# The low part of a weight granule by an accumulating DMA instead of a subtraction on VectorE

## The chip, the cores and the metric

The kernel runs on one core of a Trainium2 chip. The metric is device time in microseconds; the median of three runs of the kernel before is 964.5 us (963.53 to 964.99). TensorE is called PE here (its weight loads PEld), VectorE DVE, ScalarE ACT, GpSimd POOL, and SyncE, which issues most DMAs, SP.

## The reference

One layer of a hybrid decoder for 512 tokens of width 1024, all in float32. The input is normalised, shifted and scaled to `h`; one wide projection gives the inputs of two mixers (a chunkwise mLSTM with 4 heads, a differential attention with 8) and of their gates; both are normalised, gated, projected and merged.

```python
h = rmsnorm(x, norm_g[l]) * (1.0 + scale[:, None]) + shift[:, None]
proj = h @ w_in[l]
(qm, km, vm, om, zm, im, fm, qa, ka, va, za, gm, ga) = jnp.split(proj, split_idx, axis=-1)
...
ym = hm @ w_proj_m[l]
...
ya = ha @ w_proj_a[l]
y = jax.nn.sigmoid(gm) * ym + jax.nn.sigmoid(ga) * ya
x = x + gate[:, None] * (y @ w_out[l])
return rmsnorm(x, final_g)
```

## The kernel before

Products are made from a high and a low part of each operand. The high part is the float32 value rounded to the type that PE reads (float32r), the low part is the value less its high part; three products (high by high, high by low, low by high; lines 135 to 137, `mm3`) stand for one in float32.

Weights come in granules of 128 x 1024 numbers (512 KB). A granule of `w_in` is 128 columns and the whole contraction (`proj_b`, 24 products of 512 columns) or 256 columns and half the contraction (`proj_v`, 48 products of 256 columns); those of the two output projections are of the same size (`attn_proj`, `proj_m`). The first eight granules of `w_in` belong to the first two attention heads and are split by code of their own (lines 581 to 617). The other 128 go through `split_granule` (line 149): SP loads `raw` (line 146), ACT casts it to `whi` (line 100), DVE subtracts `whi` from `raw` and writes `wlo` (line 118). Each of the three tiles has three buffers in the pool `stg`, so a granule can be prepared while PE works on the two before it. The eight granules of `w_out` are split at the end of the kernel by `out_weights`, which calls `split` itself.

The program is written in the order of the granules; the attention heads and the mLSTM run as generators beside it and hand in a piece of work at each `tick`. A scheduler of the framework then sets each engine's queue by readiness and priority (the split of a granule is emitted at high priority), and each engine works its queue in order. POOL has little to do: masks on the bias tiles (`bt`, line 224) and on the mLSTM's weights (`wt`, line 766), and some memsets (`sw`, line 461).

Of the kernel before, what the change touches and what calls it, by code (L numbers as in the profile page):

```python
# [9 lines left out]
F32 = mybir.dt.float32  # L10
F32R = mybir.dt.float32r
AF = mybir.ActivationFunctionType
ALU = mybir.AluOpType
# [3 lines left out]
P = 128  # L17
# [18 lines left out]

# granules of the combined input projection, in the order of use: ("B", col) covers 128
# columns and the whole contraction, ("A", col, half) 256 columns and half the contraction,
# ("F", k) the columns of the first pair of attention heads and one block of the contraction
def _granules():  # L40
# [25 lines left out]
def hybrid_block_kernel(ctx: ExitStack, tc: tile.TileContext, xT, x, c, wada2, wada, win, wif, wpm, wpa, wout,  # L66
# [41 lines left out]

    # not before what is being emitted now on the same engine
    def pin(inst, eng):  # L110
# [4 lines left out]
    def split(hi, lo, src, eng="act", scale=None):  # L115
        copy_r(eng, hi, src, scale)
        if scale is None:
            recent["dve"] = nc.vector.tensor_tensor(lo, src, hi.bitcast(F32), ALU.subtract)  # L118
        else:
            nc.vector.scalar_tensor_tensor(lo, src, scale, hi.bitcast(F32), ALU.mult, ALU.subtract)  # L120

    # products of the heads keep their order of issue among themselves; the projections fill in
    last = [None]
# [20 lines left out]
    def load_granule(src):  # L144
        raw = stg.tile([P, D], F32, tag="raw", name=nm("raw"))
        nc.sync.dma_start(raw, src)
        return raw

    def split_granule(src):
        raw = load_granule(src)  # L150
        hi = stg.tile([P, D], F32R, tag="whi", name=nm("whi"))
        lo = stg.tile([P, D], F32R, tag="wlo", name=nm("wlo"))
        with tc.high_priority():
            split(hi, lo, raw, eng="act")
        return hi, lo
# [11 lines left out]

# [1 line left out]
    crow = stg.tile([1, D], F32, tag="raw", name="crow")  # L169
# [23 lines left out]

    # 1 / sqrt(scale * ms + eps) times -2 / scale: table value and one Newton step
    def rstd(ms_ps, scale, r=None, in_turn=None):
# [32 lines left out]

# [1 line left out]
    # silu(c) on every partition, in halves  # L230
    csl = sb.tile([P, D], F32, tag="v", bufs=2, name="csl")
    csl_done = []
    idle = core_ps()

    # products without a reader: the clock of the array stays up while the input is on its way
    def keep_warm(n, after=None):
# [24 lines left out]

    # the table of the reciprocal root comes in while x is on its way
    warm = const.tile([P, 1], F32, name="warm")
# [14 lines left out]

    # the vector engine takes its part of what leads to a block of h in this order
    mod_last = [x_sum]  # L280
# [34 lines left out]

    # x times -norm_g / 2, one block of the columns
    def x_gain(k):
# [6 lines left out]

# [1 line left out]
    toe_d = dram.tile([AH, P, RL], F32, name="toe_d")  # L326
# [11 lines left out]
    h_lo = const.tile([P, NK, S], F32R, name="h_lo")  # L338
    # out^T block: 128 columns of the projection on partitions, tokens along the free axis
    def proj_b(col, between=None):  # L340
# [23 lines left out]

    # tokens on partitions, 256 columns along the free axis; hi and lo parts [P, 4, 256]
    def proj_v(col, half, pss):
# [17 lines left out]

# [1 line left out]
    KOFF = {0: 0, 1: 512, 3: 896, 2: 1152}  # L386
    QOFF = [0, 128, 384, 768]
    LO, HI = slice(0, 64), slice(64, 128)

    # per map m the high and low parts of -q/8 stacked on the partitions; the high part at 64 m  # L390
    def evac_qa(ps):
# [7 lines left out]

    # the high part of k on both halves of the partitions, and the low parts of the two maps  # L400
    def evac_ka(ps):
# [96 lines left out]

# [1 line left out]
    acol = const.tile([P, NT * MH], F32, name="acol")  # L500
    me_d = dram.tile([MH, 2 * S], F32, name="me_d")

    def if_gates():
        # columns 0: f, 32: i, 64: low part of f, 96: low part of i
        wraw = stg.tile([P, D], F32, tag="raw", name="wraw_if")
# [20 lines left out]
        for _ in range(2):  # L526
            yield
        # tokens on the partitions for what follows
        ps = core_ps()
# [5 lines left out]
        yield  # L535
        # log_sigmoid(f) = min(f, 0) - log1p(exp(-|f|)), log1p(e) = 2 atanh(e / (2 + e))
        nc.scalar.activation(e, f, AF.Abs)
# [37 lines left out]

# [1 line left out]
    fq = [acc_ps() for _ in range(2)]  # L577
# [71 lines left out]

    # merge gates: 1 + tanh is twice the sigmoid; they wait in DRAM  # L650
    gt_d = dram.tile([16, P, S], F32, name="gt_d")
# [14 lines left out]

# [1 line left out]
    for p in range(1, 4):  # L668
# [18 lines left out]

    # half the gate as a row in DRAM
    gate_d = dram.tile([8, P], F32, name="gate_d")
# [6 lines left out]

# [1 line left out]
    ya_d = dram.tile([8, P, S], F32, name="ya_d")  # L698
# [12 lines left out]

# [1 line left out]
    JOFF = [0, 512, 896, 1152]  # L713
# [42 lines left out]
    def mlstm_core(h, q, k, v, hv):  # L756
        # stabilised weights exp(a_s - M_t), zero for s > t
        mt = sb.tile([P, S], F32, tag="me", bufs=2, name=nm("mt"))
        et = sb.tile([P, S], F32, tag="me", bufs=2, name=nm("et"))
        nc.sync.dma_start(mt, me_d[h:h + 1, 0:S].to_broadcast([P, S]))  # L760
        nc.sync.dma_start(et, me_d[h:h + 1, S:2 * S].to_broadcast([P, S]))
        wt = sb.tile([P, 1408], F32, tag="p", bufs=PB, name=nm("wt"))
        for j in range(NT):
            w = S - JT[j]
            ws = wt[:, JOFF[j]:JOFF[j] + w]
            nc.gpsimd.affine_select(ws, mt[:, JT[j]:S], [[1, w]], ALU.is_ge, BIG, base=JT[j] - P * j,
                                    channel_multiplier=-1)
            nc.scalar.activation(ws, ws, AF.Exp, scale=-1.0, bias=acol[:, j * MH + h:j * MH + h + 1])
        yield
        sw = sb.tile([P, 2, 1408], F32R, tag="sw", name=nm("sw"))  # L770
        sh, sl = sw[:, 0, :], sw[:, 1, :]
        for j in range(NT):
            w = S - JT[j]
            js = slice(JOFF[j], JOFF[j] + w)
            ps = core_ps()
            jb = slice(j * P, j * P + P)
            for kk in range(2):
                mm3(ps[:, 0:w], (k[kk][0][:, jb], k[kk][1][:, jb]), (q[kk][0][:, JT[j]:S], q[kk][1][:, JT[j]:S]),
                    kk == 0, kk == 1, head=True)
            nc.vector.tensor_mul(wt[:, js], ps[:, 0:w], wt[:, js])  # L780
            split(sh[:, js], sl[:, js], wt[:, js], eng="act")
            if j > 0:
                nc.vector.tensor_add(wt[:, JT[j]:S], wt[:, JT[j]:S], wt[:, js])
            yield
        dh, dl = tmp(dt=F32R), tmp(dt=F32R)
        split(dh, dl, wt[:, 0:S], eng="dve")
        yield
        ps = out_ps()
        inorder(nc.tensor.matmul(ps, ones_r, dh, start=True, stop=False))
        inorder(nc.tensor.matmul(ps, ones_r, dl, start=False, stop=True))  # L790
        rd = sb.tile([P, S], F32, tag="me", bufs=2, name=nm("rd"))
        nc.scalar.activation(rd, ps, AF.Abs)
        nc.vector.tensor_max(rd, rd, et)
        nc.vector.reciprocal(rd, rd)
        while len(v) < 2:
            yield
        for d in range(4):
            ps = out_ps()
            vd = slice((d % 2) * P, (d % 2) * P + P)
            for j in range(NT):  # L800
                js = slice(JOFF[j], JOFF[j] + S - JT[j])
                mm3(ps[:, JT[j]:S], (v[d // 2][0][:, j, vd], v[d // 2][1][:, j, vd]), (sh[:, js], sl[:, js]),
                    j == 0, j == NT - 1, head=True)
            t = sb.tile([P, S], F32, tag="z", bufs=8, name=nm("h"))
            nc.vector.tensor_mul(t, ps, rd)
            hv.append(t)
            yield
# [21 lines left out]

    # ym becomes what the other heads and the attention branch bring to the merge  # L830
    def premerge(b, g):
# [8 lines left out]

    # the output weights stay on chip; the input h makes room for some of them
    wo = [None] * NK
# [18 lines left out]

    # the projection of the head before, as its parts come up
    def fill():
# [53 lines left out]

# [1 line left out]
    gf = sb.tile([P, 2, D], F32, tag="v", bufs=2, name="gf")  # L919
# [142 lines left out]
```

## Time and profile before

| | |
|---|---|
| runs | 964.99, 963.53, 964.50 us |
| span of the profiled execution | 960.5 us |
| its granted TensorE clock, mean | 0.997 |
| busy: PE, DVE, ACT, POOL | 947.8, 603.9, 457.3, 17.0 us |
| DMA | 114.95 MB, mean 120 GB/s |

The profiled execution is one of its own; its span runs from the first to the last instruction, and its time around that span isn't told. The three runs lie 3.0 to 4.5 us above the span, the median 4.0 us. In the rows, "[1.2 <-ACT whi]" at the end of a line is idle time of the engine before the instruction and what ended it; a DMA share is the mean busy share of the core's 16 DMA engines.

### The profile page before, as it was taken

What the parts mean: (1) busy time and instruction counts of PE and PEld (TensorE: products, weight loads), DVE (VectorE), ACT (ScalarE), POOL (GpSimd) and SP (SyncE); (2) the same over time, 40 slices, a digit from 0 to 9 for tenths busy, and PEclk for the clock granted to TensorE, in tenths of its full rate; (3) what the DMA queues carried; (4) which work ended last, traced back from release to release, by engine and by line L of the source; (5) the groups of instructions that cost most, each with busy time, mean ns of one, the idle gap of its engine ahead of it and who ended that gap; (6) DMA issues with size and microseconds to landing.
All of it is one profiled execution on the core that took longest, in us unless ns stands there. A gap on an engine that the chain in (4) does not pass through costs nothing.

```text
span 960.5 us, 12250 instructions
## 1 busy us (share of the span) xinstructions
PE 947.8 (99%) x4735; PEld 782.3 (81%) x4735; DVE 603.9 (63%) x975; ACT 457.3 (48%) x741; POOL 17.0 (2%) x40
## 2 busy tenths in 40 slices
PE   7999999999999999999999999999999999999997
PEld 4886877887787788888888888898888888888886
DVE  7965777867755537433648535486554876738944
ACT  7455776766556644322336333363223642226422
POOL 0000000000001000000000000000000000000000
PEclk9999999999999999999999999999999999999999
DMA  9871313333422243342222222223132234335421
GB/s 346 308 226 67 116 66 109 128 132 121 131 78 88 87 166 111 132 141 100 88 89 88 89 87 100 76 89 109 68 109 69 86 110 148 118 129 203 148 67 66
DMA packets 40659, 114.95 MB, mean 120 GB/s; under 512 B 8289, under 2 KB 8553, under 8 KB 39578
## 3 DMA queue, kind: packets, MB, share of 16 engines
q1 hardware_dynamic: 40010, 113.11, 35.1%
q10 hardware_dynamic: 592, 1.07, 0.4%
q8 instruction: 37, 0.61, 0.3%
q14 instruction: 20, 0.16, 0.1%
HBM read 106.78 MB, written 10.00 MB: 122 GB/s over the span
## 4 chain that ended last, share of the span: by engine, by line
PE 97%; DMA 1%; ACT 1%; DVE 0%; SPq 0%; issue 0%
PE acc L135 27%; PE acc L136 27%; PE acc L137 26%; PE core L135 4%; PE core L136 4%; PE core L137 4%; PE core L439 2%; PE core L438 2%; PE core L468 1%; DMA relt<-in_relb_dram 1%; DMA xt<-in_xT_dram 0%; PE core L238 0%; PE core L488 0%; PE core L489 0%; SPq L174 0%; PE core L331 0%
## 5 line engine op out<-in xcount | busy, mean ns | idle before, releaser
L135 PE MATMUL acc<-h_hi,whi 128*128 128x512 f32 x688 | 274.4, 399 | 0.3 <-DVE qk L407 0.3
L118 DVE TENSOR_TENSOR wlo<-raw,whi 128x1024 fp32r<-128x1024 f32 x129 | 157.7, 1223 | 179.4 <-ACT whi L100 171.3
L100 ACT CAST whi<-raw 128x1024 fp32r<-128x1024 f32 x129 | 135.3, 1049 | 282.6 <-PE acc L136 224.3
L136 PE MATMUL acc<-h_lo,whi 128*128 128x512 f32 x656 | 259.4, 395 | 0.0
L137 PE MATMUL acc<-h_hi,wlo 128*128 128x512 f32 x656 | 259.1, 395 | 0.0
L135 PEld LDWEIGHTS acc<-h_hi,whi 128*128 128x128 f32 x688 | 129.0, 188 | 32.5 <-issue 1.5
L137 PEld LDWEIGHTS acc<-h_hi,wlo 128*128 128x128 f32 x656 | 123.0, 187 | 29.9
L136 PEld LDWEIGHTS acc<-h_lo,whi 128*128 128x128 f32 x656 | 123.1, 188 | 27.5 <-issue 0.4
L135 PE MATMUL acc<-whi,h_hi 128*128 128x256 f32 x352 | 99.6, 283 | 0.0
L137 PE MATMUL acc<-whi,h_lo 128*128 128x256 f32 x352 | 98.9, 281 | 0.0
L136 PE MATMUL acc<-wlo,h_hi 128*128 128x256 f32 x352 | 98.8, 281 | 0.0
L136 PE MATMUL acc<-hl,whi 128*128 128x512 f32 x192 | 74.8, 390 | 0.0
L135 PE MATMUL acc<-hh,whi 128*128 128x512 f32 x192 | 74.8, 390 | 0.0
L137 PE MATMUL acc<-hh,wlo 128*128 128x512 f32 x192 | 74.8, 389 | 0.0
L135 PEld LDWEIGHTS acc<-whi,h_hi 128*128 128x128 f32 x352 | 66.3, 188 | 1.8 <-issue 0.8
L136 PEld LDWEIGHTS acc<-wlo,h_hi 128*128 128x128 f32 x352 | 66.3, 188 | 0.7
L137 PEld LDWEIGHTS acc<-whi,h_lo 128*128 128x128 f32 x352 | 66.3, 188 | 0.0
L441 DVE CUSTOM_DVE_ANT_0 pt<-core,bt 128x128 f32<-128x128 f32 (+3 forms) x64 | 30.3, 487 | 30.1 <-PE core L439 29.9
L443 ACT ACTIVATE pt<-pt,mn 128x128 f32<-128x128 f32 (+3 forms) x64 | 35.6, 558 | 19.8 <-DVE mn L441 19.3
L137 PEld LDWEIGHTS acc<-hh,wlo 128*128 128x128 f32 x192 | 36.1, 188 | 7.6
L135 PEld LDWEIGHTS acc<-hh,whi 128*128 128x128 f32 x192 | 36.1, 188 | 7.4
L136 PEld LDWEIGHTS acc<-hl,whi 128*128 128x128 f32 x192 | 36.1, 188 | 7.3
(276 smaller groups left out, 1362.0 us busy)
## 6 DMA issues: line engine op xcount, KB each, us to landing
raw<-in_win_dram SPq DMA_DIRECT2D x112, 512.0 KB, 3.4
wa<-in_wada_dram SPq DMA_DIRECT2D x8, 1024.0 KB, 7.0
raw<-in_wpm_dram SPq DMA_DIRECT2D x16, 512.0 KB, 3.4
raw<-in_wada_dram SPq DMA_DIRECT2D x8, 512.0 KB, 3.3
raw<-in_wpa_dram SPq DMA_DIRECT2D x8, 512.0 KB, 3.5
raw<-in_wout_dram SPq DMA_DIRECT2D x8, 512.0 KB, 3.2
gt_d<-tmp SPq DMA_DIRECT2D x12, 256.0 KB, 2.2
toe_d<-rev_d SPq DMA_DIRECT2D x8, 320.0 KB, 6.4
```

Source lines behind the costliest of these rows:

```text
L100: recent["act"] = nc.scalar.copy(dst, src)
L118: recent["dve"] = nc.vector.tensor_tensor(lo, src, hi.bitcast(F32), ALU.subtract)
L135: a = nc.tensor.matmul(ps, lhs[0], rhs[0], start=start, stop=False)
L136: b = nc.tensor.matmul(ps, lhs[l[0]], rhs[l[1]], start=False, stop=False)
L137: c = nc.tensor.matmul(ps, lhs[r[0]], rhs[r[1]], start=False, stop=stop)
L438: inorder(nc.tensor.matmul(ps, q[m][:, qs], kh[m][:, 0:wn], start=True, stop=False))
L439: inorder(nc.tensor.matmul(ps, q[m][a, qs], kl[a, 0:wn], start=False, stop=True))
L441: nc.vector.tensor_tensor_reduce(pp, ps[:, 0:w], bt[:, S - w:S], 1.0, BIG, ALU.add, ALU.min, mn[:, qb, m:m + 1])
L443: nc.scalar.activation(pp, pp, AF.Exp, scale=-1.0, bias=mn[:, qb, m:m + 1], accum_out=ls[:, qb, m:m + 1])
L468: inorder(nc.tensor.transpose(ps[:, n:n + P], pt[:, 0, o:o + P], ident))
```

## The change

In `split_granule` the call of `split` is taken apart. ACT casts `raw` to `whi` as before. Then ACT writes the negated high part into `wlo` (an activation with scale -1), and a DMA that POOL issues reads the same granule from DRAM a second time and adds it onto `wlo`. DVE's subtraction is gone, and `raw` has one reader left. The eight granules of the first heads and those of `w_out` are split as before. Comments are taken out elsewhere, and lines behind 157 have numbers that are higher by 3.

```diff
     def split_granule(src):
         raw = load_granule(src)
         hi = stg.tile([P, D], F32R, tag="whi", name=nm("whi"))
         lo = stg.tile([P, D], F32R, tag="wlo", name=nm("wlo"))
         with tc.high_priority():
-            split(hi, lo, raw, eng="act")
+            recent["act"] = nc.scalar.copy(hi, raw)
+            nc.scalar.activation(lo, hi.bitcast(F32), AF.Copy, scale=-1.0)
+            nc.gpsimd.dma_start(lo, src, accum_op=ALU.add)
         return hi, lo
```

ACT's queue before, from the first granule behind the first heads (`qk` are the parts of the first heads' queries and keys, `acc` the PSUM banks that they are read from, `v` the values):

```order
L100 CAST whi_663<-raw_661 128x1024
L395 ACTIVATE qk_576<-acc_198 64x512
L395 ACTIVATE qk_579<-acc_198 64x512
L405 CAST qk_583<-acc_200 64x512
L406 CAST qk_583<-acc_200 64x512
L100 CAST v_606<-core_202 128x512
L100 CAST v_606<-core_203 128x512
L405 CAST qk_587<-acc_200 64x512
L100 CAST whi_729<-raw_727 128x1024
L406 CAST qk_587<-acc_200 64x512
```

The second granule's cast stands between the two casts of `qk_587`.

The same piece of ACT's queue now (L155 is the cast of a granule, L156 the negation):

```order
L155 CAST whi_663<-raw_661 128x1024
L398 ACTIVATE qk_576<-acc_198 64x512
L156 ACTIVATE wlo_664<-whi_663 128x1024
L398 ACTIVATE qk_579<-acc_198 64x512
L408 CAST qk_583<-acc_200 64x512
L409 CAST qk_583<-acc_200 64x512
L100 CAST v_606<-core_202 128x512
L100 CAST v_606<-core_203 128x512
L408 CAST qk_587<-acc_200 64x512
L409 CAST qk_587<-acc_200 64x512
L155 CAST whi_730<-raw_728 128x1024
```

A negation has come between the first two L398, and the second granule's cast now follows the pair of casts of `qk_587`.

POOL's queue before, in the later attention heads (`bt` is a head's bias tile, `sw` holds a head's transposed weights, `wt` the mLSTM's):

```order
L224 AFFINE_SELECT bt_2745<-bt_2745 128x128
L461 MEMSET sw_2312 128x2x128
L461 MEMSET sw_2663 128x2x128
L461 MEMSET sw_2990 128x2x128
L766 AFFINE_SELECT wt_3783<-mt_3779 128x512
```

It goes from head to head with nothing between.

The same place in POOL's queue now (L157 is the accumulating DMA):

```order
L227 AFFINE_SELECT bt_2775<-bt_2775 128x128
L157 DMA wlo_2089<-in_win_dram 128x1024
L157 DMA wlo_2153<-in_win_dram 128x1024
L464 MEMSET sw_2336 128x2x128
L157 DMA wlo_2204<-in_win_dram 128x1024
L157 DMA wlo_2250<-in_win_dram 128x1024
L157 DMA wlo_2298<-in_win_dram 128x1024
```

The DMAs of the granules stand between the masks and memsets, so each waits for what POOL has ahead of it.

## Rows read from the trace of the kernel before

**Rows 1.** Page: busy time of the engines, and the chain that ended last.

```profile
PE 947.8 (99%) x4735; PEld 782.3 (81%) x4735; DVE 603.9 (63%) x975; ACT 457.3 (48%) x741; POOL 17.0 (2%) x40
PE 97%; DMA 1%; ACT 1%; DVE 0%; SPq 0%; issue 0%
```

**Rows 2.** Windows: stretch, its length, busy us (instructions), clock, DMA share, GB/s.

```profile
0.00:60.00 60.00, 53.84 (x238) 40.49 (x239) 49.10 (x87) 33.72 (x48) 2.69 (x10) 0.97 0.88 308
60.00:130.00 70.00, 69.66 (x352) 54.40 (x351) 45.48 (x107) 46.20 (x99) 1.74 (x4) 1.00 0.32 106
910.00:960.50 50.50, 44.35 (x216) 36.97 (x214) 23.64 (x46) 12.67 (x29) 0.00 (x0) 0.98 0.20 67
```

**Rows 3.** Waits of PE: us in total, times, longest.

```profile
PE core L247 <- DVE crow L244: 4.6, 1, 4.6
...
PE acc L135 <- DVE qk L407: 0.3, 1, 0.3
```

**Rows 4.** Page, groups: the subtraction and the cast; busy, mean ns | idle before.

```profile
L118 DVE TENSOR_TENSOR wlo<-raw,whi 128x1024 fp32r<-128x1024 f32 x129 | 157.7, 1223 | 179.4 <-ACT whi L100 171.3
L100 ACT CAST whi<-raw 128x1024 fp32r<-128x1024 f32 x129 | 135.3, 1049 | 282.6 <-PE acc L136 224.3
```

**Rows 5.** Timeline, attention output projection, ACT and DVE: start, us, instruction.

```profile
397.19 1.05 ACT L100 CAST whi<-raw 128x1024 fp32r<-128x1024 f32 x1 [3.06 <-PE acc L136]
402.63 1.05 ACT L100 CAST whi<-raw 128x1024 fp32r<-128x1024 f32 x1 [4.39 <-PE acc L136]
408.07 1.05 ACT L100 CAST whi<-raw 128x1024 fp32r<-128x1024 f32 x1 [4.38 <-PE acc L136]
...
398.28 1.23 DVE L118 TENSOR_TENSOR wlo<-raw,whi 128x1024 fp32r<-128x1024 f32 x1 [0.17 <-ACT whi L100]
```

**Rows 6.** Windows of tile `whi` alone (PE, PEld, DVE, ACT); ACT's count is casts.

```profile
130.00:350.00 220.00, 155.51 (x540) 95.55 (x540) 35.43 (x29) 30.39 (x29) 1.00 0.34 110
350.00:390.00 40.00, 37.60 (x173) 27.79 (x171) 8.57 (x7) 7.31 (x7) 1.00 0.40 134
390.00:430.00 40.00, 36.39 (x124) 22.65 (x124) 8.58 (x7) 7.53 (x8) 1.00 0.40 140
...
495.00:550.00 55.00, 50.45 (x216) 35.78 (x215) 11.11 (x10) 10.49 (x10) 1.00 0.29 96
...
610.00:670.00 60.00, 55.96 (x235) 39.30 (x234) 13.45 (x11) 11.53 (x11) 1.00 0.27 88
...
735.00:800.00 65.00, 59.22 (x245) 41.20 (x245) 14.68 (x12) 12.61 (x12) 1.00 0.29 97
...
855.00:910.00 55.00, 48.83 (x157) 29.26 (x156) 8.54 (x7) 8.41 (x8) 1.00 0.50 168
```

**Rows 7.** Page: main DMA queue; loads with KB each and us to landing.

```profile
q1 hardware_dynamic: 40010, 113.11, 35.1%
...
raw<-in_win_dram SPq DMA_DIRECT2D x112, 512.0 KB, 3.4
wa<-in_wada_dram SPq DMA_DIRECT2D x8, 1024.0 KB, 7.0
```

**Rows 8.** DMA from 855 to 910 us: loads of 512 KB, us to landing.

```profile
raw<-in_wpm_dram SPq DMA_DIRECT2D x4, 512.0 KB, 5.2
```

**Rows 9.** Timeline of ACT and DVE at the first granules behind the first heads.

```profile
59.55 1.05 ACT L100 CAST whi<-raw 128x1024 fp32r<-128x1024 f32 x1 [4.55 <-PE core L136]
...
62.61 0.59 ACT L395 ACTIVATE qk<-acc 64x512 fp32r<-64x512 f32 x1 [1.52 <-DVE qk L396]
...
68.47 0.69 DVE L407 TENSOR_TENSOR qk<-acc,qk 64x512 fp32r<-64x512 f32 x1
```

**Rows 10.** Timeline of ACT, DVE and PE around 184 us, an attention head.

```profile
179.55 1.35 ACT L100 CAST sw<-core 128x512 fp32r<-128x512 f32 x3
...
183.36 1.02 DVE L118 TENSOR_TENSOR sw<-core,sw 128x384 fp32r<-128x384 f32 x2
...
184.00 0.39 PE L135 MATMUL core<-sw,v 128*128 128x512 f32 x1
```

**Rows 11.** Timeline of POOL and ACT, a memset ahead of a granule's DMA.

```profile
223.62 0.31 POOL L461 MEMSET sw<- 128x256 f32 x1 [12.16 <-DVE wlo L118]
...
221.29 1.05 ACT L100 CAST whi<-raw 128x1024 fp32r<-128x1024 f32 x1 [3.04 <-PE acc L136]
```

## The prediction

> **What bounds the kernel now.** I read the busy shares and the chain of waits first: TensorE (PE) is busy for 99% of the span and holds 97% of the chain that ended last [rows 1]. The waits of PE say the same from the other side: after the start-up only one wait is left, 0.3 us for a VectorE (DVE) subtraction at 69 us, beside 4.6 us at the start [rows 3]. The windows show where PE's 12.7 us of idle time lie: 6.2 us in the first 60 us, 0.3 us up to 130 us and 6.2 us behind 910 us [rows 2]. From 130 to 910 us PE has no gap at all. So DVE's subtractions of weights, 129 of 1.22 us [rows 4], 128 of which the change removes, stand beside PE and end nothing, but for that wait. The next question is how early they are: what matters is not their price but the time between the free buffer and PE's first use of the low part.
>
> I read that from the stretch of the attention output projection. ScalarE (ACT) casts a granule every 5.44 us, and each cast starts when PE lets go of the old content of its buffer (the releaser is L136, the last product that reads it) [rows 5]. There are three buffers, so PE works through two other granules before it comes to the new one: 2 x 5.44 = 10.9 us behind the cast's start. A granule is 24 products in 5.44 us, 0.23 us each, and the low part is read by the third: 10.9 + 0.45 = 11.3 us. The cast takes 1.05 us and the subtraction is done at 398.28 + 1.23, 2.3 us behind the cast's start. Some **9.0 us of slack** stand behind it.
>
> **The change part by part.**
>
> *The subtraction goes.* 128 x 1.223 us = 156.5 us off DVE's 603.9. PE never waits for them, so this is worth nothing on the path, with one exception. At 60 us ACT stands idle for 1.5 us because DVE puts a weight subtraction ahead of the first L396; and a cast of weights stands between the two L405/L406 casts whose subtraction (L407, 68.47 us) PE waits for [rows 9]. In the new order both are gone: the negation falls into ACT's idle time, and the next granule's cast comes behind the pair. PE's 0.3 us wait can go: **-0.3 us**, bounds -0.3 and 0.
>
> *ACT negates.* 128 instructions of the cast's shape on the same engine, 1.05 us each: 134 us more, 457 becomes 592 us, or 62% of the span. Most of it lies in idle time: before a cast, ACT waits for PE anyway, 3 to 4.4 us a granule in this stretch [rows 5]. What hangs on ACT are the attention heads: a negation that falls between the casts of `sw` (L470's split) and PE's use of them delays the head. The closest place is at 184 us: ACT's three casts end at 180.9, DVE's last two subtractions begin at 183.36, and PE starts on the first part at 184.00 [rows 10]. There DVE, not ACT, is the late one, and it gets 1.2 us a granule back. Bounds: nothing, and 8 heads x 1.05 = 8.4 us if each negation were paid. Near the first, since ACT is 2.4 us ahead of DVE at the tightest place: **+0.5 us**.
>
> *The accumulating DMA.* It starts behind cast and negation, 2.1 us and a hand-over, say 2.2 us, behind the start of the cast. So it has 11.3 - 2.2 = **9.1 us to be issued by GpSimd (POOL), land and be seen by PE**. This trace has no accumulating DMA and no DMA issued by POOL. Nearest rows: a plain load of the same 512 KB lands in 3.4 us, one of 1024 KB in 7.0 us, in the start-up at 88% DMA share [rows 7, 2]. The main queue's 113.11 MB take 35.1% of 960.5 us, 337 us, so 0.524 MB (512 KB) hold the 16 engines for 1.56 us [rows 7]. The accumulation reads weights and old low part, and writes: I take one more pass, 3.1 us of the engines. It also meets the load of the next `raw`, which the cast has just released and which goes out at the same time: another 1.56 us. So 3.4 + 1.56 + 1.56 = **6.5 us**. Bounds: 3.4 (a plain load), and for what no row tells, POOL's work on the descriptors and the pace of the addition, an estimate of four times that, 13.6. I take 6.5, since the second pass is sure and the rest is not.
>
> Beside it, the Trainium skill ("Collectives: The Full Stack", section "The bandwidth ceiling: the fold count and why AG ≠ RS ≠ AR") says that the addition in a DMA engine costs no time of its own, and that what halves the rate is the second source read. By it the second pass is the whole price and the sum stays as it is; no run here shows it yet.
>
> At 6.5 us it hides, with 2.6 us to spare, if the room is the same elsewhere. It is: five stretches (350 to 430, 495 to 550, 610 to 670, 735 to 800 and 855 to 910) hold 7 + 8 + 10 + 11 + 12 + 8 = 56 casts in 315 us [rows 6], 5.63 us each, so by the same rule a room of 2 x 5.63 + 0.45 - 2.2 = 9.5 us. Elsewhere heads stretch it: 29 casts in 220 us between 130 and 350 us [rows 6], 7.6 us each, a room of 13.4 us. **Nothing on the path** there.
>
> The 16 engines are the second resource. From 390 to 430 us they are busy for 0.40 x 40 = 16 us, and 8 more transfers of 3.1 us make 41: just full. From 855 to 910 us it is 27.5 + 25 = 52 of 55 [rows 6]. There a plain load already takes 5.2 us to land [rows 8], 1.8 us over the usual. With twice that queue the accumulation comes to some 9.5 to 10 us, 0.4 us past the room. With three buffers a granule that is late by d costs d/3 (three granules make one turn of the buffers): with 8 granules about 1 us. **+1.0 us**; bounds 0 and 6 (another 2 us late).
>
> *POOL's queue.* The DMAs stand in program order with POOL's memsets and masks, some of which wait for other engines. At 223.6 us a memset of `sw`, released by DVE, stands just ahead of the DMA of the granule that is cast at 221.3 us, whose negation would be done at 223.5 [rows 11]. It costs 0.4 us of a room of 13 us: nothing. What is queued behind a DMA that waits for its negation are the masks of the mLSTM weights, with 1 or 2 us at stake for ACT, not for PE.
>
> *Raw buffers.* The subtraction no longer reads `raw`, so each load can go out 1.3 us earlier. It was never waited for: nothing.
>
> Sum: 960.5 - 0.3 + 0.5 + 1.0 = 961.7 us of span. The median of the runs, 964.5, is 4.0 us above the profiled span (the runs lie 3.0 to 4.5 us above it); with that, **965.7 us**, 0.13% over the time before. A measurement of this kernel can tell about 0.2% (1.9 us) from no change, so this counts as the same.
>
> **The rivals.**
>
> *The accumulation is longer than its room.* Decides from about 9.1 us of issue and landing, in the 56 tight granules. PE then waits at the third product of each, and a turn of three buffers is cast, negation, DMA and PE's own granule: each granule costs (L - 9.5)/3. At L = 10 us some 10 us, at 12 us (2.5/3) x 56 = 47 us: 965.7 + 47 = 1013 us. For it: POOL's part is unknown, and the first granule, whose cast is at 59.55 us [rows 9], comes right behind the busiest stretch of the DMA engines [rows 2]. Against it: two plain passes are 5 us. Chance 0.27 for L up to 12 us.
>
> *The DMA engines fill.* If an accumulation holds them for four quiet passes, 6.2 us, 128 of them are 794 us. Of the 337 us before, the first 60 us hold 0.88 x 60 = 53, so 284 + 794 = 1078 us have to fit behind 60 us: a span of 1138, a time of 1142 us. Decides from about 3.1 us, where two stretches are full, and holds everywhere from 6 us on. Between lies L = 14 us without full engines: (4.5/3) x 56 = 84 us from the tight granules and, with the room of 13.4 us, (0.6/3) x 72 = 14 us from the others, 1064 us. For it: a DMA that adds may be far from a plain one's pace. Against it: nothing in the trace. Chance 0.19 for more than 1013 us.
>
> *It gains.* DVE's relief would have to shorten PE's path. PE's 6.2 us at the start and the 6.2 us behind 910 us [rows 2] belong to work that the change leaves as it is, so only 0.3 us are to be had: 964.2, not a faster kernel. Chance for over 0.2%: 0.04, for what I do not see.
>
> **How the numbers follow.** Forecast, hidden: 0.50, own range 963 to 967. Long accumulation: 0.27, 967 to 1013. Full engines or L beyond 12 us: 0.19, above 1013. Gain: 0.04. The range runs from 963.0 to 1013.0; 0.19 is left out above and some 0.03 below. Faster 0.04, same 0.50, slower 0.27 + 0.19 = 0.46.
>
> **What would show it.** DVE's busy time near 447 us and ACT's near 592; a landing of `wlo` by the new DMA of 5 to 8 us; PE's waits without a DMA of `wlo`; DMA share in the tight stretches between 0.6 and 1. If PE's waits name `wlo` for more than 2 us in total, the first rival is there, and its turn of buffers must show as casts more than 5.5 us apart between 390 and 430 us. If the 40 slices of the DMA show 9 throughout, it is the second. The prediction is wrong if issue and landing pass 9 us, whatever the reason.

## The result, and the profile after

The changed kernel takes 971.5 us (969.8 to 974.4) against 964.3 (963.5 to 965.0): a ratio of 1.0077, interval 1.0064 to 1.0090. It is 7.1 us slower, well over the 0.2% that can be told. The forecast was 965.7 in a range of 963 to 1013: the time lies inside the range, but above the 963 to 967 of the case that was forecast, the hidden DMA.

The page of the changed kernel, busy time and the chain that ended last, beside [rows 1]:

```profile
PE 953.4 (98%) x4735; PEld 785.0 (81%) x4735; DVE 462.0 (48%) x847; ACT 573.3 (59%) x869; POOL 124.5 (13%) x168
PE 94%; DMA 3%; issue 2%; ACT 1%; SPq 0%; DVE 0%; POOL 0%; POOLq 0%
```

DVE is relieved by 142 us, ACT gets 116 us, POOL 108 us, and none of them is near its limit. The chain has 3% of DMA, where it had 1%. The waits of PE name it (us in total, times, longest), beside [rows 3]:

```profile
PE core L250 <- DVE crow L247: 4.5, 1, 4.5
PE acc L137 <- DMA wlo<-in_wpm_dram: 2.7, 2, 2.5
PE acc L137 <- DMA wlo<-in_win_dram: 1.4, 1, 1.4
```

Three waits for the low part, out of 128 granules. The windows say where they lie (columns as in [rows 2]):

```profile
60.00:130.00 70.00, 68.50 (x330) 53.01 (x329) 34.59 (x96) 52.17 (x104) 9.01 (x13) 0.95 0.71 174
130.00:350.00 220.00, 220.00 (x1051) 173.34 (x1050) 113.53 (x264) 165.81 (x286) 30.61 (x43) 1.00 0.72 175
390.00:430.00 40.00, 40.00 (x200) 34.03 (x200) 8.80 (x13) 18.41 (x21) 5.97 (x7) 1.00 0.93 224
855.00:910.00 55.00, 52.32 (x224) 41.80 (x223) 33.17 (x47) 35.80 (x45) 6.84 (x8) 0.98 0.92 248
```

In the middle PE has no gap, even from 390 to 430 us, where the DMA engines are busy for 93% of the time. The losses lie in the first and the last row, and in both the granted clock is below 1 too: the trace has TensorE at half its clock (1.2 in place of 2.4 GHz) for 6.8 us from 88.7 us on and for 3.4 us from 907.9 us on, behind the wait that ends at 907.4. The profile of the kernel before has neither. The first one, in a closer window: first the row of the kernel before, then that of the changed one.

```profile
88.00:96.00 8.00, 8.00 (x31) 5.15 (x29) 4.85 (x21) 3.94 (x10) 0.00 (x0) 1.00 0.06 23
```

```profile
88.00:96.00 8.00, 8.00 (x20) 5.69 (x21) 3.81 (x23) 2.41 (x11) 0.24 (x1) 0.57 0.49 102
```

PE is busy throughout in both and does 31 products in the one, 20 in the other. "Busy" hides a halved clock; the column behind POOL's shows it.

The best single view of such a small difference is the lag of PE. Both kernels issue 4735 products; the table takes the start of the n-th (counted from 0) from the trace of each kernel and subtracts the start that it has in the kernel before (us; e1 to e9 are the experiments below):

| product | start before | after | e1 | e2 | e3 | e7 | e8 | e9 |
|---|---|---|---|---|---|---|---|---|
| 270 | 66.1 | 0.7 | 1.4 | 1.9 | 1.1 | 2.4 | 2.2 | 1.2 |
| 300 | 73.6 | 1.9 | 0.9 | 3.0 | 0.6 | 1.9 | 2.8 | 2.5 |
| 500 | 111.5 | 4.9 | 2.4 | 4.5 | 0.6 | 6.8 | 2.8 | 5.5 |
| 1900 | 390.4 | 4.9 | 2.4 | 4.5 | 0.7 | 7.1 | 2.8 | 5.5 |
| 4300 | 859.2 | 4.9 | 2.4 | 4.5 | 0.7 | 7.1 | 2.8 | 5.5 |
| 4500 | 905.4 | 9.8 | 5.6 | 6.1 | 0.7 | 7.1 | 4.5 | 8.4 |
| end of span | 960.5 | 10.3 | 6.0 | 6.5 | 1.1 | 7.5 | 5.0 | 8.8 |

Read down the column "after": 0.7 us at the start-up (it differs from execution to execution, 0.7 to 2.4 us in the first row); +1.2 at the first split granule (a wait of 1.45 in place of 0.25); +3.0 at the halved clock; nothing at all from 111 to 859 us; +4.9 at the end, of which 0.2 and 2.5 are waits and 1.7 is the halved clock, taken as half of its 3.4 us. (The profiled execution of before lies 2 us under its median, that of after 1 us over; so 10.3 us of spans stand for 7.1 us of medians.)

### The profile page after: what moved, and what is told of

It reads as the page before. It is cut to its first block, busy times and chain, and to the rows that moved or that the text cites. A ratio compares the mean times of both kernels' runs of the same rounds, so it can differ in the third digit from the quotient of the medians.

```text
span 970.7 us, 12533 instructions
## 1 busy us (share of the span) xinstructions
PE 953.4 (98%) x4735; PEld 785.0 (81%) x4735; DVE 462.0 (48%) x847; ACT 573.3 (59%) x869; POOL 124.5 (13%) x168
## 3 DMA queue, kind: packets, MB, share of 16 engines
q0 software_dynamic: 18432, 67.12, 39.8%
## 4 chain that ended last, share of the span: by engine, by line
PE 94%; DMA 3%; issue 2%; ACT 1%; SPq 0%; DVE 0%; POOL 0%; POOLq 0%
PE acc L135 26%; PE acc L136 26%; PE acc L137 26%; PE core L135 3%; PE core L136 3%; PE core L137 3%; PE core L442 2%; PE core L441 2%; DMA wlo<-in_wpm_dram 1%; DMA wlo<-in_win_dram 1%; PE core L471 1%; DMA xt<-in_xT_dram 1%; DMA bt<-toe_d 1%; PE core L241 0%; SPq L177 0%
## 5 line engine op out<-in xcount | busy, mean ns | idle before, releaser
L155 ACT CAST whi<-raw 128x1024 fp32r<-128x1024 f32 x128 | 134.3, 1049 | 250.3 <-PE acc L136 228.9
L157 POOL DMA_DIRECT2D wlo<-in_win_dram x104 | 89.1, 856 | 528.5 <-ACT wlo L156 489.0
L156 ACT ACTIVATE wlo<-whi 128x1024 fp32r<-128x1024 f32 x128 | 134.9, 1054 | 0.5
L726 DVE SCALAR_TENSOR_TENSOR tmp<-tmp,sm,tmp 128x509 f32<-128x509 f32 (+2 forms) x48 | 35.9, 749 | 46.4 <-ACT tmp L723 45.5
L908 DVE SCALAR_TENSOR_TENSOR h<-tmp,h 128x512 f32<-128x512 f32 x16 | 11.1, 692 | 68.8 <-ACT tmp L907 68.8
```

The costliest lines, as they stand in the source:

```text
L155: recent["act"] = nc.scalar.copy(hi, raw)
L156: nc.scalar.activation(lo, hi.bitcast(F32), AF.Copy, scale=-1.0)
L157: nc.gpsimd.dma_start(lo, src, accum_op=ALU.add)
L726: nc.vector.scalar_tensor_tensor(y[:, sft:S], xc[:, 0:S - sft], w(j), y[:, sft:S], ALU.mult, ALU.add)
L908: nc.vector.scalar_tensor_tensor(hv[d], t, 1.0, hv[d], ALU.add, ALU.mult)
```

## Why those granules

The DMA queue of POOL, the landings by tensor (KB each, median us), and min/median/max of all 128 landings, then of those between 860 and 912 us:

```profile
q0 software_dynamic: 18432, 67.12, 39.8%
...
wlo<-in_win_dram POOLq DMA_DIRECT2D x104, 512.0 KB, 5.6
wlo<-in_wpm_dram POOLq DMA_DIRECT2D x16, 512.0 KB, 6.7
```

```profile
DMA to landing us min/median/max: 5.0/5.9/9.9
```

```profile
DMA to landing us min/median/max: 5.2/8.6/9.9
```

39.8% of 970.7 us, over 128, are 3.02 us of the 16 engines for one accumulation. The landings from 390 to 430 us, the tightest stretch, where the room was 9.1 us:

```profile
DMA to landing us min/median/max: 5.6/6.9/7.6
```

So at 93% DMA share the accumulation still lands inside its room. A landing of 8.6 us asks for more room than the late granules below had.

The first split granule, ACT, then POOL, then PE:

```profile
60.25 1.05 ACT L155 CAST whi<-raw 128x1024 fp32r<-128x1024 f32 x1 [4.55 <-PE core L136]
61.20 0.59 ACT L398 ACTIVATE qk<-acc 64x512 fp32r<-64x512 f32 x1
61.69 1.05 ACT L156 ACTIVATE wlo<-whi 128x1024 fp32r<-128x1024 f32 x1
...
63.06 1.00 POOL L157 DMA_DIRECT2D wlo<-in_win_dram  x1 [5.79 <-ACT wlo L156]
...
71.66 0.50 PE L137 MATMUL acc<-h_hi,wlo 128*128 128x512 f32 x1 [1.45 <-DMA wlo<-in_win_dram]
```

The negation stands 0.4 us behind the cast's end, because an evacuation of the first heads (L398) comes between. The DMA is issued at 63.06 and PE goes on at 71.66: 8.6 us, where PE came to the low part at 70.2. Between this granule's cast and its use PE has the rest of the first heads and sixteen products of the gates, not two granules: 10.0 us from the start of the cast, where the prediction had 11.3. And the DMA goes out 2.8 us behind that start, not 2.2. So its room is 7.1 us, not 9.1, and this DMA, the first of all, takes 8.6 us to land.

The last granules, ACT and POOL at 895 to 902 us:

```profile
894.89 1.05 ACT L100 CAST h_hi<-raw 128x1024 fp32r<-128x1024 f32 x1 [3.62 <-DMA raw<-in_wout_dram]
895.85 1.05 ACT L155 CAST whi<-raw 128x1024 fp32r<-128x1024 f32 x1
896.79 0.59 ACT L930 ACTIVATE gm<-acc 128x512 f32<-128x512 f32 x1
897.28 1.05 ACT L156 ACTIVATE wlo<-whi 128x1024 fp32r<-128x1024 f32 x1
...
898.62 0.85 POOL L157 DMA_DIRECT2D wlo<-in_wpm_dram  x1 [7.71 <-ACT wlo L156]
```

ACT stands still for 3.6 us for a load of `w_out`, in order, and the cast of a granule waits behind it. In the kernel before that cast starts at 887.89:

```profile
887.89 1.05 ACT L100 CAST whi<-raw 128x1024 fp32r<-128x1024 f32 x1 [1.50 <-PE acc L136]
```

With PE's lag of 4.9 us that would be 892.8; here it is 895.85, 3 us late. The transfer is slow too, at a DMA share of 92% (855 to 910 us above): issued at 898.62, PE goes on at 907.38, 8.8 us.

```profile
907.38 0.50 PE L137 MATMUL acc<-hh,wlo 128*128 128x512 f32 x1 [2.47 <-DMA wlo<-in_wpm_dram]
```

PE came to this low part at 904.9, so the late start had left it 6.3 us of room. The third wait, 0.2 us, is that of the granule issued at 884.07: 9.5 us of room, 9.6 of landing. Late start and slow landing together make the waits at the end.

## The experiments

The theory: the accumulation is free wherever it has its room, and the 7 us come from granules that lack it (the first and the last few), and from a halved clock that these waits bring about. The rivals: 128 negations and transfers cost a little each everywhere; the halved clock has a cause of its own. The kernel before ran beside each set, with medians of 964.1 (e1 to e4), 964.3 (e5 to e8) and 964.2 us (e9 to e12).

**e1: the first granule by subtraction.** `n` counts the calls of `split_granule`.

```diff
         with tc.high_priority():
-            recent["act"] = nc.scalar.copy(hi, raw)
+            if n == 0:
+                split(hi, lo, raw, eng="act")
+            else:
+                recent["act"] = nc.scalar.copy(hi, raw)
...
```

> The changed kernel, with the first granule of split_granule (the one that TensorE waits for at 71.7 us) split by VectorE's subtraction as before and the other 127 by the accumulating DMA. Theory (a few granules lack the room, and the halved clock at 88.7 to 95.5 us is a knock-on of this first wait): the wait of 1.45 us goes back to about 0.25, the 3.4 us of the halved clock go too, so 7.1 - 1.2 - 3.4 = 2.5 us over the kernel before, about 966.9 us (966.2 to 967.6). Rival A (the halved clock comes from the new order of ScalarE's and GpSimd's work, not from the wait): only 1.2 us go, 5.9 over before, about 970.3 us. Rival B (128 negations and transfers each cost a little everywhere): within 0.5 us of the changed kernel, 971.0 or more.

966.9 us (963.8 to 969.5), ratio 1.0024, 1.0011 to 1.0037. The size is the one forecast, its parts are not. The wait at 72 us is gone. But the clock is halved for 3.4 us from 89.2 us on without that wait, and the waits at the end add up to 2.6 us:

```profile
PE acc L137 <- DMA wlo<-in_wpm_dram: 2.6, 2, 1.7
```

**e2: the last four granules by subtraction.** As e1, with `n >= 124`.

> The changed kernel, with the last four granules (in_wpm of the last head, 880 to 908 us) split by subtraction and the other 124 by the accumulating DMA. Theory: the waits of 0.2 and 2.5 us for wlo at 893 and 907 us go, and with them the halved clock at 907.9 to 911.3 us (1.7 us): 7.1 - 4.2 = 2.9 us over the kernel before, about 967.2 us (966.5 to 968.0); the first wait and the halved clock at 88 us stay. Rival A (the DMA engines are full in this stretch whoever makes the low part, and the loads of wout are late anyway): 2 us or less go, 969.3 or more. Rival B (a cost spread over all granules): 970.8 or more.

968.8 us (967.6 to 969.7), ratio 1.0047, 1.0035 to 1.0059: 1.6 us more than forecast. The waits for `in_wpm` are gone, but the granule before them now waits, 1.3 us at 888.8 us. Its negation had stood on ACT behind a cast for `w_out` that waited for its load.

```profile
PE acc L137 <- DMA wlo<-in_win_dram: 2.6, 2, 1.3
```

**e3: both.** As e1, with `n == 0 or n >= 124`; 123 granules still accumulate.

> The changed kernel, with the first granule and the last four by subtraction, the 123 between by the accumulating DMA. Theory: 123 accumulations hide wholly, so no wait for wlo over 0.5 us is left and the granted clock is halved at no place where it was not before; 964.0 us, within 0.8 of the kernel before. Rival B (a cost spread over all granules, by ScalarE's negations or by the engines of the DMA): 968 us or more.

964.1 us (962.3 to 967.5), ratio 0.9999, 0.9988 to 1.0010. PE has no wait for `wlo`, and no halved clock between 21 and 959 us. 123 negations and 123 accumulating DMAs cost nothing that can be told, by the interval 1 us at most; this settles the rival of a cost spread over all granules. Against e3, e1 has the end added (2.9 us) and e2 the first granule with its wait at 889 us (4.7 us); 7.6 us in all, about the 7.1 of the change. The two parts are not clean: PE's queue is the same in e1 and e3, and yet the profile of e1 has 3.4 us at half clock near 89 us, which the granules at the end can't have brought.

**e4: the negation without the DMA.**

```diff
             nc.scalar.activation(lo, hi.bitcast(F32), AF.Copy, scale=-1.0)
-            nc.gpsimd.dma_start(lo, src, accum_op=ALU.add)
+            recent["dve"] = nc.vector.tensor_tensor(lo, raw, lo.bitcast(F32), ALU.add)
```

> ScalarE's negation alone: the low part is made by the cast, the negation on ScalarE and an addition of the raw granule on VectorE, with no accumulating DMA. It prices the 128 negations by themselves (some 135 us more on ScalarE, VectorE as before). Theory: 964.3 us, within 0.6 of the kernel before, since the chain is only 1.1 us longer than the old one and every room is 7.6 us or more. Rival B (the negations take ScalarE from work that TensorE waits for): 967 to 971 us.

965.5 us (964.3 to 966.4), ratio 1.0016, 1.0007 to 1.0024: 1.3 us over the kernel before, more than the theory's 0.6 and less than the rival's 967 to 971 us. DVE's addition takes what the subtraction took (1221 ns) but waits for the negation. PE names no wait for either; the lag grows by 0.6 us between 170 and 196 us, where an attention head stands in another order, and by 0.2 at the end. As e3 has nearly all the negations at no cost, they aren't the price of the change; where e4's 1.3 us come from is not settled.

**e5: a late low part without a DMA.** In the kernel before, the first granule's subtraction is held behind a chain on POOL.

```diff
+            if count[0] == 1:
+                copy_r("act", hi, raw)
+                nc.gpsimd.tensor_copy(lo, hi.bitcast(F32))
+                for _ in range(8):
+                    nc.gpsimd.memset(lo.bitcast(F32), 0.0)
+                recent["dve"] = nc.vector.tensor_tensor(lo, raw, hi.bitcast(F32), ALU.subtract)
```

> The kernel before, with no accumulating DMA at all; only the first granule's low part is held back by a chain of nine passes over its buffer on GpSimd (some 10 us from the cast's end at 60.6 us) before VectorE's subtraction, so that TensorE waits for it at about 71 to 72 us as in the changed kernel. It tells a wait by itself from the transfers. Theory (the wait brings the halved clock at about 89 us, by moving the heads' products against the clock's steps): wait of 1 to 2 us and a halved clock of 3.4 us or 6.8 us behind it, 3 to 5 us over the kernel before, 967.1 to 969.1. Rival (the halved clock there needs the transfers, or ScalarE's negations, that change the order of TensorE's work): the wait alone, 1 to 2 us over before, 965.1 to 966.1, with no halved clock at 85 to 96 us.

963.6 us (962.0 to 964.9), ratio 0.9993, 0.9984 to 1.0002. It missed its aim: the low part is ready only at 74.3 us, but the scheduler knew of the chain and put the heads' products, at 76.9 us in the changed kernel, at 72.2 us. PE did not wait. So a wait without a DMA was not tried after all. In the changed kernel the scheduler had left the heads' products behind the granule, and PE waited; that it prices the DMA too low is likely, but not shown.

**e6: every accumulation twice.**

```diff
             nc.gpsimd.dma_start(lo, src, accum_op=ALU.add)
+            nc.gpsimd.dma_start(lo, src, accum_op=ALU.add)
```

> Every accumulating DMA is issued twice, one behind the other onto the same low part, so that the low part holds the raw granule once too often; it doubles the way L and the engines' time of an accumulation (3.02 us of 16 engines measured) together. By the rule of room alone (L about 2 x 5.9 = 11.8 us, a third of 11.8 - 9.5 for each of 56 tight granules) it costs 43 us over the changed kernel, about 1015 us. By the engines (128 x 6.0 us = 773 us, with the 284 us of plain transfers behind 60 us, on 16 engines) the span cannot be under 60 + 1057 = 1117 us, about 1120 to 1150 us. Theory: the engines decide, 1117 us or more.

1329.9 us (one run). Over 1117, but not by the engines, which are busy for 81 to 86% in the long stretches. The timeline of POOL shows the cause:

```profile
704.06 0.86 POOL L158 DMA_DIRECT2D wlo<-in_win_dram  x1 [7.26 <-DMA wlo<-in_win_dram]
704.60 1.20 POOL L157 DMA_DIRECT2D wlo<-in_wpm_dram  x1
712.34 0.86 POOL L158 DMA_DIRECT2D wlo<-in_wpm_dram  x1 [6.55 <-DMA wlo<-in_wpm_dram]
```

The second DMA of a granule (L158) waits on POOL for the first to land, and the next granule's first stands behind it in the queue. So at most two of these DMAs are under way, the second of one granule and the first of the next: 8.3 us from one L158 to the next here, 9.4 on average over all 128 (71.9 to 1266.3 us). It says nothing on the two rules that it was to tell apart.

**e7: more room.** In `proj_b` and `proj_m` all products with the low part come last; 128 granules accumulate.

```diff
-            mm3(ps, (hi[:, ksl], lo[:, ksl]), (h_hi[:, k, :], h_lo[:, k, :]), k == 0, k == NK - 1)
+            nc.tensor.matmul(ps, hi[:, ksl], h_hi[:, k, :], start=(k == 0), stop=False)
+            nc.tensor.matmul(ps, hi[:, ksl], h_lo[:, k, :], start=False, stop=False)
...
+        for k in range(NK):
+            last_mm[0] = nc.tensor.matmul(ps, lo[:, k * P:(k + 1) * P], h_hi[:, k, :], start=False, stop=(k == NK - 1))
```

> The changed kernel with all 128 accumulating DMAs, but in proj_b and proj_m TensorE takes all the products with the high part of a granule first and those with the low part last: the same products, and 3.5 us more room for the low part. Theory (a few granules lack room): no wait of over 0.5 us for wlo is left at 70 us or at the end, and the time is that of the kernel with those granules subtracted, 964.0 us (963.2 to 965.8, the upper part if the clock is halved at 89 us as chance has it). Rival (what the late accumulations cost comes by the full engines, and the loads and other work behind them are late whatever TensorE's order): 967 us or more.

968.7 us (963.4 to 971.7), ratio 1.0037, 1.0023 to 1.0052. The waits for `wlo` are gone, all of them, though the DMAs land no sooner (median 6.3 us); the room was what lacked. Behind 859 us the lag doesn't grow at all. But the time has not followed: in the profiled execution the clock is halved from 80.2 to 83.6 us and from 90.5 to 97.3 us, 4.9 us of lag without any wait.

```profile
80.00:88.00 8.00, 8.00 (x30) 5.96 (x28) 1.76 (x8) 4.10 (x11) 0.86 (x1) 0.79 0.87 209
88.00:96.00 8.00, 8.00 (x21) 5.27 (x21) 4.75 (x25) 3.81 (x15) 0.85 (x1) 0.65 0.54 115
```

So the halved clock near 88 us isn't the wait's consequence alone. Here the mean granted clock of each run, which is on record, tells more than one profile: the three runs at 0.995 or more took 963.4 to 965.7 us, the nine at 0.993 or less 967.1 to 971.7. What is left of e7's loss goes with the clock.

**e8: the negation on DVE.**

```diff
-            nc.scalar.activation(lo, hi.bitcast(F32), AF.Copy, scale=-1.0)
+            nc.vector.tensor_scalar(lo, hi.bitcast(F32), -1.0, None, ALU.mult)
```

> The changed kernel with the negation on VectorE in place of ScalarE, the 128 accumulating DMAs as they are. It tells how much of the lateness at the end is the negation's place in ScalarE's queue (behind casts that wait for loads of wout) and how much the way of the transfer itself. Theory (both): the wait of 1.4 us at 72 us stays, that at 907 us gets shorter by 1 to 2 us but does not go, since the transfers there take 9 us; 969 to 970.5 us. Rival (the queue is all of it): the waits at the end go, 967.5 us. Rival (the transfer is all of it): no change, 971 to 972 us.

968.5 us (967.2 to 972.5), ratio 1.0055, 1.0038 to 1.0073, between the theory and the rival of ACT's queue. A negation is 692 ns on DVE. The waits at the end shrink from 2.7 to 1.2 us and do not go; that at 72 us is 0.9. ACT's queue is a part of the lateness, the transfer's way the other. The profiled execution has no halved clock from 22 to 961 us, though it still waits 0.9 us for the first granule; it is the fastest of the six runs.

```profile
PE acc L137 <- DMA wlo<-in_wpm_dram: 1.2, 2, 0.7
```

**e9, e10, e11: the order of PE.** What precedes the halved clock is in all kernels a stretch of fourteen narrow products of the heads. Behind it the kernel before has six products of a granule and then two more of the heads; the changed kernel, e1 to e4 and e7 have one product of the granule there, a choice of the scheduler (e8, with the negation on DVE, has four, and e5, without one, six). PE's queue before, from the end of the fourteen:

```order
L438 MATMUL core_794<-qk_598,qk_591 128x256
L439 MATMUL core_794<-qk_597,qk_591 128x256
L135 MATMUL acc_811<-h_hi,whi_807 128x512
L136 MATMUL acc_811<-h_lo,whi_807 128x512
L137 MATMUL acc_811<-h_hi,wlo_808 128x512
L135 MATMUL acc_811<-h_hi,whi_807 128x512
L136 MATMUL acc_811<-h_lo,whi_807 128x512
L137 MATMUL acc_811<-h_hi,wlo_808 128x512
L438 MATMUL core_799<-qk_602,qk_594 128x256
```

And after:

```order
L441 MATMUL core_796<-qk_598,qk_591 128x256
L442 MATMUL core_796<-qk_597,qk_591 128x256
L135 MATMUL acc_814<-h_hi,whi_809 128x512
L441 MATMUL core_801<-qk_602,qk_594 128x256
L442 MATMUL core_801<-qk_597,qk_594 128x256
L136 MATMUL acc_814<-h_lo,whi_809 128x512
```

e9 is the changed kernel and e11 is e7, each with the pair held behind the sixth product; e10 is the kernel before with the pair right behind the first.

```diff
+            if k == 1 and late:
+                issue_after(late.pop()[0], last_mm[0])
```

> The changed kernel, with one pair of the heads' products (L441/L442 of the second head's second block) held in TensorE's order behind the sixth product of the granule there, as it stands in the kernel before; in the changed kernel it stands behind the first, so that sixteen narrow products follow each other with one granule product between. Theory (the halved clock at 88 to 97 us comes of this order, which the scheduler made from the negations on ScalarE): no halved clock there, the waits of 1.4 us at 72 us and of 2 to 3 us at the end stay; 968.5 us (967.5 to 969.5). Rival (it comes of the wait before it, or of chance with either order): as the changed kernel, 971 to 972 us.

> The kernel before with the opposite: the pair of heads' products in TensorE's order behind the first product of the granule, as in the changed kernel; nothing else is changed, no negation, no accumulating DMA. Theory (order): the halved clock at 85 to 96 us comes in some executions, the runs spread upward, median 964.3 to 966.5, single runs up to 968. Rival (the transfers or the first wait are needed): as the kernel before, 963.9 to 964.7, with its spread.

> The changed kernel with all 128 accumulating DMAs, the products with the low part last (as in the run that had no wait for wlo left and lost 5 us by the halved clock alone), and the pair of heads' products held behind six products of the granule. Theory (order): neither waits nor the halved clock are left, 964.2 us (963.3 to 965.5). Rival (chance, or the transfers): as without the hold, 967.5 to 969.5 us.

e9: 970.3 us (964.7 to 971.1), ratio 1.0050, 1.0033 to 1.0068. e10: 964.5 (964.2 to 966.2), 1.0007, 0.9998 to 1.0016. e11: 965.6 (962.4 to 968.8), 1.0015, 1.0002 to 1.0029. e9 and e11 lie between theory and rival, e10 is within both. The medians of e9 and e11 are 1.2 and 3.0 us under those of the kernels without the hold, but the profiles of both still have 6.8 us at half clock near 88 us (e11 3.4 us more from 77.7 us on), and e10's has none. First e9's row, then e10's:

```profile
88.00:96.00 8.00, 8.00 (x20) 5.54 (x20) 2.86 (x18) 2.98 (x13) 0.81 (x1) 0.57 0.56 121
```

```profile
88.00:96.00 8.00, 8.00 (x32) 5.62 (x32) 4.26 (x26) 3.40 (x11) 0.00 (x0) 1.00 0.20 66
```

The order alone does not decide it: e9 and e11 have the order of the kernel before, and the halved clock. That it has no part isn't shown. Two of e10's eleven runs, without any accumulating DMA, have a mean clock of 0.993 (965.9 and 966.2 us); all 76 runs of the kernel before in the three sets have 0.995 or more, and all four of the changed kernel 0.994 or less. That mean takes in the start-up and the end, so it doesn't say where those two runs lost it.

**e12: the second transfer by itself.** The kernel before, and each granule copied once more to a spare buffer in DRAM.

```diff
             split(hi, lo, raw, eng="act")
+            nc.gpsimd.dma_start(dram.tile([P, D], F32, tag="spare", bufs=4, name=nm("spare")), src)
```

> The kernel before, with VectorE's subtraction as it was, and beside it GpSimd's queue copies each of the 128 granules once more, plainly, from its place in DRAM to a spare buffer in DRAM, for which nothing waits. It prices a second transfer of each granule and the 0.86 us of issue on GpSimd by themselves. Theory (a transfer that nobody waits for costs nothing, also where the engines are nearly full): 964.3 us (963.5 to 965.3). Rival (the load alone makes the raw loads at the end late): 966 us or more, with PE waits for raw granules or for casts behind them at 880 to 910 us.

1148.8 us (1147.8 to 1150.0), ratio 1.1914, 1.1899 to 1.1929. The design was at fault: only the four spare buffers hold these copies back, so POOL issued all 128 within the first 226 us, and the loads of the start-up came late (product 270 of PE by 172 us). It can't tell what the same load costs when it is spread out; e3 does. It has one clean number, the price of a plain copy from DRAM to DRAM on POOL's queue: 16.1% of 1146.2 us, over 128, are 1.44 us of the engines.

```profile
q0 software_dynamic: 4096, 67.12, 16.1%
...
spare<-in_win_dram POOLq DMA_DIRECT2D x104, 512.0 KB, 14.3
```

**What stays open: the halved clock near 88 us.** Twelve profiles side by side:

| kernel | accumulating DMAs near 80 us | granule products between | PE's wait for the first `wlo` | at half clock near 88 us |
|---|---|---|---|---|
| before | no | 6 | - | none |
| e4 | no | 1 | - | none |
| e5 | no | 6 | - | none |
| e10 | no | 1 | - | none |
| after | yes | 1 | 1.5 us | 6.8 us |
| e1 | yes | 1 | - | 3.4 us |
| e2 | yes | 1 | 1.3 us | 3.4 us |
| e3 | yes | 1 | - | none |
| e7 | yes | 1 | - | 6.8 us, and 3.4 us from 80.2 on |
| e8 | yes | 4 | 0.9 us | none |
| e9 | yes | 6 | 1.5 us | 6.8 us |
| e11 | yes | 6 | - | 6.8 us, and 3.4 us from 77.7 on |

No column decides: e1 and e3 are the same program up to 880 us and differ. With the DMAs it came in six profiles of eight, without in none of four. A profile is one execution; the spread of the runs (963.4 to 971.7 for e7, 962.3 to 965.6 for the kernel before in its three sets, but for two runs up to 966.0) says that it comes and goes. I take it for a matter of when PE enters the narrow products, which the DMAs move by a few tenths to 2 us, but that is argued only, and the lag alone doesn't bear it out: at product 300 it is 1.9 us in the changed kernel and in e10, and only the former has the halved clock. The one at 907.9 us is open as well. It follows the wait of 2.5 us, but was seen once; e1 and e9, with waits of 1.7 and 1.6 us at that granule, have none there. A shift of PE's schedule without wait or DMA would tell; it wasn't tried.

## Why the prediction was right and wrong

*The frame held.* PE bounds the kernel, DVE's 142 us are worth nothing, and what counts is the room of the low part. From 111 to 859 us the accumulation is free, in the tight stretches too.

*The accumulating DMA.* Landing 6.5 us forecast, 5.9 measured (5.0 to 9.9); 3.1 us of the engines forecast, 3.02 measured. A plain copy by the same queue, though to DRAM and in fewer packets, takes 1.44 (e12). The Trainium skill ("Collectives: The Full Stack", section "The bandwidth ceiling: the fold count and why AG ≠ RS ≠ AR") has, for a collective's ring, the second source read as the price of an addition on the way, a factor of two. The trace agrees as to the size, 3.02 / 1.44 = 2.1; that the read is the reason isn't shown here.

*The step that failed is "if the room is the same elsewhere. It is".* The room was taken from averages over stretches of 40 to 65 us, with the rule of two granules ahead. It holds in the middle. But the first split granule had 7.1 us in place of 9.1, and the one that PE wants at 904.9 us 6.3. The prediction's own [rows 9] had the first one's cast, and the first rival even named it, but no room was worked out for it. Issue and landing passed the 9.1 us in three DMAs of 128 (9.5, 9.6 and 9.9), and only one of these has a wait, of 0.2 us; 3.9 of the 4.1 us of waits came where the room was short, at landings of 8.6 and 8.7.

*That the range held is luck in part.* Its upper bound stands for 56 tight granules that all wait. That didn't come: between 390 and 430 us the casts stay 5.44 us apart. Three single granules came, and a halved clock that no case had.

*The term of +1.0 us at 855 to 910 us was too small.* The full engines came (92%, where the prediction's sum gives 95), and the landing there has a median of 8.6 us and a maximum of 9.9, where "9.5 to 10 us" was forecast. But the lateness isn't shared among three buffers. Nearly all of it fell on one granule, whose cast stood behind a cast for `w_out` that waited for its load: 2.7 us of waits and 1.7 us of halved clock behind them. That is within the term's bounds of 0 to 6. The prediction asked what a negation delays on ACT, not what delays a granule's cast and negation there.

*-0.3 us came* where no wait replaced it: the lag falls by 0.5 us between 66 and 74 us in e1 and e3. In the changed kernel it is lost to the longer wait in its place.

*+0.5 us for ACT did not come* at the heads: PE's lag doesn't grow between 111 and 859 us.

*The clock was missing.* No term of the sum and no rival had it, though 4.7 us of the two profiles' 10.3 lie there (3.0 near 88 us, 1.7 behind 908). A shift by a microsecond was priced at a microsecond.

*4.0 us beside the span* mixed two things. In the later runs each execution of the kernel before lies 2.0 us above its own span (964.7 with 962.7); the other 2 us were that the profiled one lies that much under the median.

*Of the signs named,* the landing and the DMA share (0.77 to 0.93 in the tight stretches) came as said. DVE's busy time is 462 us in place of 447 and ACT's 573 in place of 592; the sums left out that instructions of one engine overlap at their ends (a cast at 60.25 of 1.05 us, the next instruction at 61.20). "PE's waits name `wlo` for more than 2 us" came at 4.1, but the casts more than 5.5 us apart, which were to go with it, did not: it is the first rival's wait, in three places in place of 56. The second rival (full engines) did not come: PE runs through.

## What to carry to other kernels

An asynchronous step that is far longer than what it replaces has to be checked against the room of every instance, the first and the last above all: there the pipeline isn't in its steady state, and the transfer is slowest where other loads crowd. Leaving five granules of 128 on the old way made the change free (e3). Giving the consumer its late operand last removed every wait for it (e7), though not the halved clock. Neither made the kernel faster than before, because VectorE was not the bound. When a wait of a microsecond moves a schedule, look at the granted clock behind it before the sum is closed.

## What the runs showed of the hardware

- An accumulating DMA of 512 KB from DRAM into SBUF, issued by POOL, lands in 5.0 to 9.9 us, median 5.9, beside other traffic. It holds POOL for 0.86 us and the 16 engines for 3.02 us, with 144 packets; a plain copy from DRAM to DRAM by the same queue is 1.44 us with 32 packets.
- Most plain loads beside it got slower, without PE waiting in the middle: `raw` from `in_win` 3.4 us before [rows 7], now 4.0. Near the end it is mixed: `raw` from `w_proj_m` went from 5.2 us [rows 8] to 3.4.

```profile
raw<-in_win_dram SPq DMA_DIRECT2D x112, 512.0 KB, 4.0
```

- A DMA on POOL that waits for another's landing blocks the queue behind it: 9.4 us for each granule in e6, on average.
- A negation of 128 x 1024 numbers is 1054 ns on ACT and 692 on DVE, where the two-operand subtraction is 1223 [rows 4].
